# One output projection over all eight head pairs in a decoder trunk, without partial sums

## The chip, the core and the metric

The kernel runs on one core of a Trainium2 chip. The metric is device time of one launch in microseconds (us). The core has a matmul engine (PE, with its weight loads shown apart as PEld), three engines for elementwise work (DVE, ACT, POOL), and SP, which here issues nearly all DMAs between HBM and the on-chip SBUF. Matmuls write into PSUM, which has eight banks of 128 x 512 float32 here. Each engine works through its own instructions in order and waits on semaphores of the others.

## The reference, cut to what matters

Sequence 512, width 1024, 16 heads of 64, MLP width 4096, two layers. Layer 0 mixes by pooling, layer 1 by stick-breaking attention; each is followed by a squared-ReLU MLP.

```python
for layer in range(DEPTH):
    h = rms_norm(x, mix_pre_g[layer])
    if layer < N_A:
        m = pool_mixer(h, pool_w[layer], pool_scale[layer])
    else:
        q = jnp.matmul(h, w_q[j]).reshape(B, S, N_HEADS, HEAD_DIM).transpose(0, 2, 1, 3)
        o = stick_breaking_attention(q, k, v)
        m = jnp.matmul(o.transpose(0, 2, 1, 3).reshape(B, S, HD), w_o[j])
    x = x + rms_norm(m, mix_post_g[layer])
    h = rms_norm(x, mlp_pre_g[layer])
    x = x + rms_norm(sq_relu_mlp(h, w_up[layer], w_down[layer]), mlp_post_g[layer])
    if layer == N_A - 1:
        kv = jnp.matmul(rms_norm(x, kv_norm_g), w_kv)...
```

The change is in how `m = o @ w_o`, the norm behind it and the start of the second MLP are laid out.

## The kernel before, in words

Every float32 matrix product is made of three matmuls on rounded operands: each operand is split into a high part (an ACT cast, `hi`) and a low part (a DVE subtraction, `lo`), and `mm3` adds hi·hi, hi·lo and lo·hi. So each weight of 128 x 1024 costs one load, one ACT cast and one DVE subtraction before PE may use it. Where a weight is scaled by a norm's gains, there is a scaling ahead of that.

Weights reach PE in three ways. `weight` (line 139) loads and splits one on its way into a ring of four tiles (`place`, lines 171-189). Some are split beforehand during the first MLP (`split_apart`, lines 319-343: up to 31 steps, one behind each of its block products), stored to HBM as two parts (`keep_parts`) and later only loaded (`make`, lines 347-352); `SOON` says for how many of the eight head pairs the query and key weights go this way. The rest, listed in `LATE`, are loaded, scaled, split and, if marked `s`, stored during attention, at places that a table gives.

That table, `ATT_ORDER` (lines 55-66), is the order of attention written out by hand for PE, ACT, DVE, POOL and SP at once. A row is one head pair. `S` is the scores of a pair on PE, `G` their sigmoids on ACT, `X` a scan and `M` a product on DVE (for each of two heads), `Q`/`J` the projections of the next pair's queries and keys on PE and `q`/`j` their copies out of PSUM, `T` the transposes, `A` the product with the values, `a` its split into the tile `ohl`. `L`, `g`, `W`, `w`, `s` are a late weight's load, scaling (DVE), high part (ACT), low part (DVE) and store. `R` loads two rows of norm gains. `N`, `V`, `v`, `F` make the values in the first two rows.

The output projection before is done in three portions. `O00` to `O03` multiply the pairs 0 and 1 with their two weights for the four token tiles of 128, in the fifth pair's row; `o00` to `o03` copy the results to SBUF (`y`). `O10` to `O13` do pairs 2 and 3 in the last row, and `o1x` adds them to `y` on DVE. Behind the table the pairs 4 to 7 follow, tile after tile (lines 1337 to 1391), and are added to `y` once more. Each tile then goes through `Update` (lines 457 to 534): squares summed on ACT, a gain on POOL or DVE (`gained`), a power on POOL (`rstd`), `sums_added` into the residual `x` with squares of it, another power, `norm`, `transpose` on PE and a `split` into `xnh`/`xnl`, from which the second MLP's first matmuls read (`up_block`, line 816; the first four blocks take the first two token tiles first, and `need(2)`, `need(3)` transpose the other two at the fourth block).

`xn3` is one tile of three slots. A slot serves in turn as the place of an `Update`'s squares and normed rows, and of the high part of a late weight that is stored.

Two engines, PE and SP, run strictly in the order in which the table and the code behind it issue; in the two MLPs a scheduler at build time chooses the order.

## Time and profile before

| | us |
|---|---|
| three timed runs | 909.95, 913.77, 914.89 (median 913.77) |
| the profiled execution's own time | 911.04 |
| its span, first to last instruction | 909.2 |
| first MLP, roughly | 50 to 340 |
| attention rows (first scores to the eighth pair's scores) | 390.1 to 531.6 |
| second MLP, first matmul | 583.8 |

The profiled execution lies 2.7 us under the median and 1.1 us over the fastest of the three, and 1.8 us of it lie outside the span. In a row of the timeline the first number is the start, the second the duration; a matmul's duration includes its way through the array, so matmuls that follow each other closely overlap, and the distance of their starts tells the rate. In a row of the windows, each engine's busy time in that stretch is followed by its number of instructions, and PEclk is the share of full clock that PE was granted.

### The profile page before, as it was taken

How to read it: one execution, taken by the hardware profiler on the slowest of the kernel's cores; microseconds unless marked ns; L12 is line 12 of the kernel's file. 1: busy time of each engine (PE TensorE's matmuls, PEld its weight loads, DVE VectorE, ACT ScalarE, POOL GpSimd, SP SyncE). 2: the span in 40 equal slices, each digit the busy share in tenths (PEclk: the TensorE clock that was granted, in tenths of full speed). 3: DMA queues.
4: the chain of work that ended last, by engine and by line, in shares of the span. 5: the costliest groups of instructions: out<-in, count | busy, mean ns of one | idle time of the engine just before them, and what ended most of it. 6: DMA issues, size and time to landing. Idle time of an engine off the chain costs nothing.

```text
span 909.2 us, 11769 instructions
## 1 busy us (share of the span) xinstructions
PE 890.8 (98%) x4522; PEld 772.5 (85%) x4522; DVE 710.8 (78%) x728; ACT 546.0 (60%) x888; POOL 90.4 (10%) x86
## 2 busy tenths in 40 slices
PE   9999999999999999999999999799999999999996
PEld 7998888888888888888887877698888888888886
DVE  5956798987988965877986897764596876967956
ACT  6667757476896847366876873356554454544632
POOL 2100000000000014000000001211130310403103
PEclk9999999999999999999999999899999999999999
DMA  7443557377695823946412126032504243133102
GB/s 287 172 178 139 185 204 260 116 269 275 241 370 209 294 99 109 375 164 255 162 47 93 47 93 231 17 112 83 207 23 162 93 139 116 47 139 115 49 22 92
DMA packets 39725, 143.09 MB, mean 157 GB/s; under 512 B 4032, under 2 KB 4506, under 8 KB 39670
## 3 DMA queue, kind: packets, MB, share of 16 engines
q1 hardware_dynamic: 39522, 142.34, 42.9%
q8 instruction: 35, 0.57, 0.3%
q14 instruction: 20, 0.16, 0.1%
q10 hardware_dynamic: 148, 0.02, 0.0%
HBM read 117.17 MB, written 25.17 MB: 157 GB/s over the span
## 4 chain that ended last, share of the span: by engine, by line
PE 79%; DVE 8%; ACT 5%; DMA 3%; issue 3%; POOL 1%; SPq 0%; POOLq 0%; DVEq 0%; ACTq 0%
PE ps L708 24%; PE ps L822 13%; PE ps L821 13%; PE ps L823 13%; PE ps L1105 3%; DMA xn<-in_wdn 2%; PE ps L446 2%; PE ps L447 2%; PE ps L445 2%; PE ps L960 2%; PE ps L1195 2%; PE ps L1244 2%; DMA w<-kept 1%; PE ps L1254 1%; PE ps L936 1%
## 5 line engine op out<-in xcount | busy, mean ns | idle before, releaser
L708 PE MATMUL ps<-w,a 128*128 128x512 f32 x1176 | 266.7, 379 | 0.3 <-ACT a L407 0.3
L821 PE MATMUL ps<-xnh,w 128*128 128x512 f32 (+1 forms) x704 | 254.0, 363 | 2.5 <-ACT xnh L407 2.5
L822 PE MATMUL ps<-xnl,w 128*128 128x512 f32 (+1 forms) x704 | 254.0, 361 | 0.1
L823 PE MATMUL ps<-xnh,w 128*128 128x512 f32 (+1 forms) x704 | 253.8, 361 | 0.0
L708 PEld LDWEIGHTS ps<-w,a 128*128 128x128 f32 x1176 | 222.0, 189 | 32.3 <-ACT a L407 0.7
L821 PEld LDWEIGHTS ps<-xnh,w 128*128 128x128 f32 x704 | 133.5, 191 | 18.5 <-ACT xnh L407 3.1
L822 PEld LDWEIGHTS ps<-xnl,w 128*128 128x128 f32 x704 | 134.2, 191 | 15.6 <-DVE xnl L408 0.3
L823 PEld LDWEIGHTS ps<-xnh,w 128*128 128x128 f32 x704 | 134.2, 191 | 15.4
L153 DVE TENSOR_TENSOR w<-raw,w 128x1024 fp32r<-128x1024 f32 x56 | 68.4, 1221 | 55.2 <-ACT w L151 55.2
L151 ACT CAST w<-raw 128x1024 fp32r<-128x1024 f32 x56 | 58.5, 1045 | 81.6 <-PE ps L823 81.5
L717 DVE TENSOR_TENSOR y<-ps,y 128x512 f32<-128x512 f32 x124 | 82.7, 682 | 20.5 <-PE ps L708 20.5
L475 POOL TENSOR_TENSOR y<-y,grow 128x512 f32<-128x512 f32 x12 | 17.4, 1454 | 542.4 <-ACT xn L411 542.4
L407 ACT CAST w<-e 128x1536 fp32r<-128x1536 f32 (+1 forms) x30 | 41.8, 1393 | 42.5 <-DVE e L681 28.9
L407 ACT CAST a<-r 128x768 fp32r<-128x768 f32 (+1 forms) x60 | 47.0, 785 | 32.5 <-DVE r L662 17.5
L408 DVE TENSOR_TENSOR w<-e,w 128x1536 fp32r<-128x1536 f32 (+1 forms) x30 | 53.8, 1794 | 10.6 <-ACT w L407 10.4
L408 DVE TENSOR_TENSOR a<-r,a 128x768 fp32r<-128x768 f32 (+1 forms) x60 | 59.1, 984 | 0.0
L1228 DVE TENSOR_TENSOR_SCAN e<-u,begin 128x1280 f32<-128x1280 f32 x16 | 45.2, 2823 | 17.1 <-ACT u L1219 16.3
L411 ACT ACTIVATE xn<-y 128x512 f32<-128x512 f32 (+1 forms) x24 | 14.9, 621 | 50.9 <-DVE y L566 28.8
L408 DVE TENSOR_TENSOR w<-xn,w 128x1536 fp32r<-128x1536 f32 (+1 forms) x20 | 33.0, 1651 | 9.5 <-ACT w L407 9.3
L408 DVE TENSOR_TENSOR w<-w,w 128x1536 fp32r<-128x1536 f32 (+1 forms) x20 | 34.5, 1727 | 6.7 <-ACT w L407 6.7
L407 ACT CAST w<-xn 128x1536 fp32r<-128x1536 f32 (+1 forms) x20 | 27.8, 1390 | 18.9 <-PE ps L708 18.9
L740 ACT ACTIVATE r<-ps 128x512 f32<-128x512 f32 x56 | 33.0, 590 | 8.6 <-PE ps L823 8.6
(180 smaller groups left out, 1295.7 us busy)
## 6 DMA issues: line engine op xcount, KB each, us to landing
raw<-in_wup SPq DMA_DIRECT2D x62, 512.0 KB, 3.7
w<-kept SPq DMA_DIRECT2D x44, 512.0 KB, 6.0
w<-in_wdn SPq DMA_DIRECT2D x8, 1536.0 KB, 7.0
xn<-in_wdn SPq DMA_DIRECT2D x8, 1536.0 KB, 6.2
kept<-wx SPq DMA_DIRECT2D x20, 512.0 KB, 5.5
kept<-apart SPq DMA_DIRECT2D x16, 512.0 KB, 6.2
apart<-in_wv SPq DMA_DIRECT2D x10, 512.0 KB, 5.3
raw<-in_wdn SPq DMA_DIRECT2D x8, 512.0 KB, 4.5
```

Source lines behind the costliest of these rows:

```text
L151: nc.scalar.copy(hi, raw)
L153: nc.vector.tensor_tensor(out=lo, in0=raw, in1=hi.bitcast(F32), op=ALU.subtract)
L407: latest["act"] = nc.scalar.copy(hi, src)
L408: latest["dve"] = nc.vector.tensor_tensor(out=lo, in0=src, in1=hi.bitcast(F32), op=ALU.subtract)
L708: nc.tensor.matmul(bank, a[:, x, q, TS[t]], by_twos(w[:, z, q], NS[0]), start=start and q == 0 and k == 0, stop=q == self.n - 1 and k == 2 ...
L717: nc.vector.tensor_tensor(out=part, in0=bank, in1=part, op=ALU.add)
L740: nc.scalar.activation(split_up(r, 256), in_order(pu, 256), ACT.Relu)
L821: nc.tensor.matmul(pu[:, cols], wh[:, k, :], xh, start=k == 0, stop=False)
L822: nc.tensor.matmul(pu[:, cols], wh[:, k, :], xl, start=False, stop=False)
L823: nc.tensor.matmul(pu[:, cols], wl[:, k, :], xh, start=False, stop=k == KC - 1)
L1105: nc.tensor.matmul(bank, a[x][q], in_turn(w[q // 2][z][:, cols], 512), start=(i == 0 or not linked) and q == 0 and n == 0, stop=q == 3 and ...
L1228: nc.vector.tensor_tensor_scan(out=e[:, ::-1], data0=us[a][:, 1:][:, ::-1], data1=begin[:, ::-1], initial=0.0, op0=ALU.mult, op1=ALU.max,)
```

## The change

All eight pairs of a token tile now go into one PSUM sum for each half of the columns. `Z` followed by a tile and two pairs (`Z034`: tile 0, pairs 3 to 4) adds those pairs to the tile's two banks. Tiles 0 and 1 are begun in the last row of the table, up to pair 6, and hold four banks; behind the table pair 7 finishes them, and tiles 2 and 3 get all eight pairs in one go. The copies and additions into `y` are gone, as is the gain on POOL: `evacuate` squares the bank on ACT and multiplies the bank by the gain row on DVE into a tile `at`.

The weights of the projection must now stay until the end, so they get places of their own: `o0`, `o1` in the four `y` tiles, `o3`, `o4` in the columns of token tiles 2 and 3 of `xnh` and `xnl`, `o5` to `o7` in attention's own tiles, and only `o2` in the ring. In `xnh` a weight's row lies in eight pieces of 128 with a step of 512 elements; `by_twos` got a case for it. `SOON` goes from 4 to 5: `q4` and `k4` are split in the first MLP, whose steps go from 31 to 33 (one earlier, one later). In `LATE`, `up2` is no longer stored but kept in the ring, `up3` is stored at the very end, and `o0` and `o1` come early.

```diff
-    S1 G1 X10 M10 X11 Q2 M11 q2 W w s J2 A0 W j2 w s L a0 L g g T10 T11
-    S2 G2 X20 M20 X21 Q3 M21 q3 W w L J3 A1 W j3 w L a1 g g T20 T21
-    S3 G3 X30 M30 X31 Q4 M31 q4 W w L J4 A2 W j4 w L a2 T30 T31
-    S4 G4 X40 M40 X41 Q5 M41 q5 W w L J5 A3 W j5 w L a3 g g O00 W w L O01 o00 T40 o01 T41 O02 W w L o02 O03 g g o03
-    S5 G5 X50 M50 X51 Q6 M51 q6 W w L J6 A4 W j6 w L a4 T50 T51
+    S1 G1 X10 M10 X11 Q2 M11 q2 W w L J2 A0 W j2 w L a0 T10 T11
+    S2 G2 X20 M20 X21 Q3 M21 q3 J3 A1 j3 a1 g g T20 T21
+    S3 G3 X30 M30 X31 Q4 M31 q4 W w L J4 A2 W j4 w L a2 g T30 T31
+    S4 G4 X40 M40 X41 Q5 M41 q5 W w L g J5 A3 j5 W w L a3 g T40 T41
+    S5 G5 X50 M50 X51 Q6 M51 q6 W w L g J6 A4 j6 W w L a4 T50 T51
     S6 G6 X60 M60 X61 Q7 M61 q7 W w L J7 A5 W j7 w L a5 T60 W T61 w L
-    S7 G7 X70 M70 O10 W w L o10 X71 O11 M71 A6 o11 W a6 w O12 W T70 o12 w R O13 T71 o13 W w W w A7 a7""".split()
+    S7 A6 G7 X70 Z002 M70 W X71 w L Z102 M71 W T70 w a6 W w R W Z034 Z134 w L T71 W w L Z055 Z155
+    W w A7 Z066 Z166 a7 W w s""".split()
...
-SOON = 4
+SOON = 5
...
-    for w in "v0 v1 up2s up3s q4 k4 q5 k5 o0 o1 q6 k6 q7 k7 o2 o3 up0 up1 o4 o6 o5 o7".split()
+    for w in "v0 v1 o0 o1 q5 k5 q6 k6 q7 k7 o2 up0 o3 o4 up1 up2 o5 o6 o7 up3s".split()
...
+        if k in (("o", 0), ("o", 1)):
+            return tiles(work, (("y0", "y1"), ("y2", "y3"))[k[1]])
+        elif k in (("o", 3), ("o", 4)):
+            return [x[:, :, TS[k[1] - 1]] for x in (xnh, xnl)]
         elif k == ("o", 5):
-            return [att_pool[0].tile([P, D], F32R, tag="ohl", bufs=6, name=name("w")) for x in "hl"]
+            return tiles(att_pool[0], "kq")
...
-        if n < 2:
+        if n < 2 or upto["L"] > len(late) - 4:
             raw = wts.tile([P, D], F32, tag="raw", bufs=2, name=name("raw"))
...
+        if len(w.shape) == 3:
+            half = w[:, 4 * (cut.start // 512) :][:, : KC // 2]
+            return half.rearrange("p (j b) c -> p b c j", j=2)
         half = w[:, NS[cut.start // 512]].rearrange("p (j i) -> p i j", j=2)
...
-        steps = [n for n in range(1, 32)] if l == 0 else []
+        steps = [n for n in range(33)] if l == 0 else []
...
+        def out_product(t, cs, halves=range(2)):
+            for n in halves:
+                if (t, n) not in sums:
+                    sums[t, n] = ps()
+                for c in cs:
+                    if c not in wos:
+                        wos[c] = get(("o", c))
+                    (lh, ll), (wh, wl) = os[c], wos[c]
+                    mm3(
+                        sums[t, n], lh[:, TS[t]], ll[:, TS[t]], by_twos(wh, NS[n]), by_twos(wl, NS[n]),
+                        c == 0, c == PAIRS - 1,
+                    )
...
+            ups = [Update(t, gpost1, None, gpre=gpre1) for t in range(T)]
+
+            def evacuate(t, n):
+                up, bank = ups[t], sums.pop((t, n))
+                up.halves = (up.halves or []) + [ap.tile([P, 512], F32, tag="at", bufs=6, name=name("at"))]
+                up.just_square(n, bank)
+                latest["dve"] = nc.vector.tensor_tensor(
+                    out=up.halves[n], in0=bank, in1=gpost1[:, NS[n]], op=ALU.mult
+                )
+
+            for t in range(2):
+                for n in range(2):
+                    out_product(t, [PAIRS - 1], [n])
+                    evacuate(t, n)
+                ups[t].factor()
+            for t in range(2):
+                ups[t].sums_added()
+                ups[t].rstd()
+            for t in range(2):
+                ups[t].norm()
+            out_product(2, range(PAIRS), [0])
+            evacuate(2, 0)
+            out_product(2, range(PAIRS), [1])
+            ups[0].transpose()
+            evacuate(2, 1)
+            ups[2].factor()
+            out_product(3, range(PAIRS), [0])
+            ups[2].sums_added()
+            ups[1].transpose()
+            evacuate(3, 0)
+            ups[2].rstd()
+            ups[2].norm()
+            out_product(3, range(PAIRS), [1])
             fill(4)
...
```

The lines of `kernel.py` below attention's table move by up to 10: `L249` before is `L258` after, `L1155` is `L1165`, `L411` is `L418`.

First place: DVE in the fifth pair's row, from the low part of the next queries on. `w<-raw` is a late weight's low part, `gc` marks a scaling, `kl` is the low part of the next keys, `ohl` that of the attention output. Before:

```order
L1168 TENSOR_TENSOR q_4109<-ps_4083,q_4109 64x512 x2
L249 TENSOR_TENSOR w_4114<-raw_3777,w_4114 128x1024
L1155 TENSOR_TENSOR kl_2960<-ps_4119,k_4155 64x512 x2
L249 TENSOR_TENSOR w_4153<-raw_3823,w_4153 128x1024
L408 TENSOR_TENSOR ohl_4165<-ps_4144,ohl_4165 128x512
L223 TENSOR_TENSOR spare_3948<-spare_3948,gc 128x1024
L223 TENSOR_TENSOR late_3994<-late_3994,gc 128x1024
L249 TENSOR_TENSOR w_4184<-spare_3948,w_4184 128x1024
L249 TENSOR_TENSOR w_4259<-late_3994,w_4259 128x1024
```

And after:

```order
L1178 TENSOR_TENSOR q_4126<-ps_4100,q_4126 64x512 x2
L258 TENSOR_TENSOR w_4131<-spare_3630,w_4131 128x1024
L230 TENSOR_TENSOR late_3680<-late_3680,gc 128x1024
L1165 TENSOR_TENSOR kl_2988<-ps_4137,k_4171 64x512 x2
L258 TENSOR_TENSOR w_4178<-late_3680,w_4178 128x1024
L415 TENSOR_TENSOR ohl_4183<-ps_4162,ohl_4183 128x512
L230 TENSOR_TENSOR raw_3964<-raw_3964,gc 128x1024
```

One scaling has moved in front of `kl`, and the row ends with one scaling in place of four instructions.

Second place: ACT at the end of the table, where the tiles 0 and 1 are squared (`stat` with the smaller number is tile 0). The waits of an instruction stand behind it; `DMAHW` is a DMA's landing. Before:

```order
L411 ACTIVATE xn_80,stat_4831<-y_2987 128x512 [waits DVE_49] x2
L411 ACTIVATE xn_80,stat_4832<-y_2988 128x512 [waits DVE_49]
L411 ACTIVATE xn_80,stat_4831<-x_69 128x512 [waits DVE_49,Activation_49] x2
L411 ACTIVATE xn_80,stat_4832<-y_2988 128x512 [waits DVE_49]
L411 ACTIVATE xn_80,stat_4833<-y_2989 128x512 [waits DVE_49]
```

And after:

```order
L414 CAST ohl_4792<-ps_4771 128x512 [waits DVE_49,PE_49]
L249 CAST xn_80<-raw_4753 128x1024 [waits DMAHW1_49]
L418 ACTIVATE xn_80,stat_4800<-ps_4620 128x512 [waits PE_49]
L418 ACTIVATE xn_80,stat_4800<-ps_4630 128x512 [waits PE_49]
L418 ACTIVATE xn_80,stat_4801<-ps_4647 128x512 [waits DMAHW3_49,DVE_49,PE_49]
L418 ACTIVATE xn_80,stat_4801<-ps_4657 128x512 [waits PE_49]
L418 ACTIVATE xn_80,stat_4800<-x_69 128x512 [waits DVE_49,Activation_49] x2
```

The cast of `up3` into a slot of `xn3` now stands ahead of the squares, and the first square of tile 1, which writes the same slot, waits for a DMA: the store of that slot. The squares of tile 0's `x` stand behind it.

Third place: SP's queue at the end of the table, from the load of the gain rows (`grow`, `spare`) on; `kept<-` is a store, `w<-kept` its load, `in_wdn` the second MLP's first down weights. Before:

```order
L131 DMA grow_4766<-in_grow 128x1024
L131 DMA spare_4768<-in_grow 128x1024
L352 DMA w_4784<-kept_3601 128x1024 x2
L352 DMA w_4828<-kept_3647 128x1024 x2
L141 DMA raw_5199<-in_wup 128x1024
L141 DMA raw_5230<-in_wup 128x1024
L645 DMA w_5040<-in_wdn 128x2x1024
L131 DMA grow_7154<-in_grow 128x1024
```

And after:

```order
L132 DMA grow_4696<-in_grow 128x1024
L132 DMA spare_4698<-in_grow 128x1024
L223 DMA raw_4728<-in_wo 128x1024
L223 DMA raw_4753<-in_wup 128x1024
L142 DMA raw_5179<-in_wup 128x1024
L203 DMA kept_4797<-xn_80 128x1024
L203 DMA kept_4797<-raw_4753 128x1024
L142 DMA raw_5210<-in_wup 128x1024
L361 DMA w_4995<-kept_4797 128x1024 x2
L132 DMA grow_7134<-in_grow 128x1024
L655 DMA w_5020<-in_wdn 128x2x1024
```

Behind the last late loads now come the store and the reload of `up3`, and the first down weights stand behind the gain row `grow_7134`, whose place is read by the out projection's last `evacuate`.

More of the change, by code (lines that the diff above doesn't have):

```diff
@@ L231, in late_high @@
         else:
-            assert key[0] == "o" and key[1] > 3 or sum(k[0] != "o" or k[1] < 4 for k in made) < ahead
+            assert not in_ring(key) or sum(map(in_ring, made)) < ahead
             for y in queue:
@@ L359, in fill @@
         for _ in range(n):
-            if queue and sum(k[0] != "o" or k[1] < 4 for k in made) < ahead and (queue[0][0][0] != "dn" or dn_pool[0]):
+            if queue and sum(map(in_ring, made)) < ahead and (queue[0][0][0] != "dn" or dn_pool[0]):
                 if not any(x["key"] == queue[0][0] for x in late) or queue[0][0] in kept:
@@ L383, in trunk @@
                     want(("q", i), wq[i], gains(C_MIX_PRE1 * KC, KC))
-                elif what == "O" and part == 0:
-                    for c in range(2 * i, 2 * i + 2):
-                        want(("o", c), wo[c])
+            want(("o", 2), wo[2])
             direct = [x for x in queue[n:] if x[2] is not None]
@@ L1050, in quarter @@
         def quarter():
-            return ap.tile([P, 4, 256], F32, tag="ohl", bufs=6, name=name("s"))
+            return ap.tile([P, 4, 256], F32, tag="ohl", bufs=7, name=name("s"))
         def form(i):
@@ L1238, in transposed @@
                 c = 0
-                turned = ap.tile([P, S], F32, tag="at", bufs=8, name=name("at"))
+                turned = ap.tile([P, S], F32, tag="at", bufs=6, name=name("at"))
                 for s in tiles:
@@ L1260, in mixed_out @@
             if p < PAIRS - 1:
-                both = ap.tile([P, D], F32R, tag="ohl", bufs=6, name=name("ohl"))
+                both = ap.tile([P, D], F32R, tag="ohl", bufs=7, name=name("ohl"))
             else:
```

94 lines of the change are left out of this document (17 added, 77 removed).

## The prediction

> **What bounds the kernel now.** I read the page's busy shares and slices first, then the windows by stage, then PE's waits.
>
> ```profile
> PE 890.8 (98%) x4522; PEld 772.5 (85%) x4522; DVE 710.8 (78%) x728; ACT 546.0 (60%) x888; POOL 90.4 (10%) x86
> PE   9999999999999999999999999799999999999996
> PEclk9999999999999999999999999899999999999999
> ```
>
> PE is busy for 98% of the span. Its 4522 matmuls are the same arithmetic after the change (192 of them are the output projection, as 8 pairs x 4 tiles x 2 halves x 3), so the change can only gain where PE stood still or was slow, and can only lose by making it stand still elsewhere. In the slices there is one such place, the 26th, where PE and its clock fall together. The windows show it by stage; the first two run from a pair's scores to the next pair's:
>
> ```profile
> 450.30:467.50 17.20, 17.20 (x103) 14.10 (x101) 16.65 (x14) 13.82 (x30) 0.00 (x0) 1.00 0.18 62
> 467.50:497.30 29.80, 28.04 (x151) 23.20 (x150) 21.76 (x18) 20.63 (x41) 0.00 (x0) 1.00 0.24 81
> 573.60:588.00 14.40, 9.15 (x37) 7.33 (x37) 10.89 (x18) 5.54 (x15) 4.11 (x5) 0.76 0.00 0
> 150.00:200.00 50.00, 50.00 (x233) 43.77 (x233) 48.60 (x47) 30.17 (x35) 0.00 (x0) 1.00 0.50 179
> ```
>
> A plain pair takes 17.2 us of unbroken PE work, with DVE close behind at 16.65. The fifth pair (467.5) takes 29.8 because `O00` to `O03` lie in it, and the stretch from 573.6 has only 9.15 us of PE work, at 0.76 of the clock. In the first MLP (last row) PE never stops although DVE is busy for 48.6 of 50 us. PE's waits name the causes:
>
> ```profile
> PE ps L446 <- DVE w L249: 2.6, 2, 1.8
> PE ps L531 <- DVE xn L522: 2.6, 1, 2.6
> PE ps L821 <- ACT xnh L407: 2.5, 1, 2.5
> ```
>
> PE waits twice for the low part of an output weight (1.8 in the fifth pair, 0.8 in the last), once for the normed rows of tile 1 before their transposes, and once for the split of these before the second MLP.
>
> **What the change removes.** The rate of PE at the end of the projection, by starts:
>
> ```profile
> 572.92 0.38 PE L445 MATMUL ps<-w,ohl 128*128 128x512 f32 x1
> 573.13 0.38 PE L446 MATMUL ps<-w,ohl 128*128 128x512 f32 x1
> 576.37 1.32 PE L531 MATMUL ps<-ident,xn 128*128 128x128 f32 x8 [2.64 <-DVE xn L522]
> 578.24 0.63 PE L447 MATMUL ps<-w,ohl 128*128 128x512 f32 x1
> 578.67 0.63 PE L445 MATMUL ps<-w,ohl 128*128 128x512 f32 x1
> 583.79 0.60 PE L821 MATMUL ps<-xnh,w 128*128 128x256 f32 x3 [2.47 <-ACT xnh L407]
> 585.32 0.42 PE L822 MATMUL ps<-xnl,w 128*128 128x256 f32 x1
> 585.53 0.42 PE L823 MATMUL ps<-xnh,w 128*128 128x256 f32 x1
> 588.12 0.28 PE L821 MATMUL ps<-xnh,w 128*128 128x256 f32 x1
> 588.23 0.28 PE L822 MATMUL ps<-xnl,w 128*128 128x256 f32 x1
> ```
>
> A 512-column matmul comes every 0.215 us at full clock and every 0.43 after the 2.64 us wait; a 256-column one every 0.21, and every 0.11 once the clock is back. So the 37 instructions of the stretch 573.6 to 588.0 (the tail of one, 8 transposes, 9 matmuls of 512, 19 of 256) are worth 0.9 + 9 x 0.216 + 19 x 0.11 = 4.9 to 5.0 us, and 14.4 - 5.0 = **9.4 us** are lost there. Afterwards tiles 0 and 1 need only pair 7 behind the table (4 x 3 matmuls, 2.6 us), and tile 2's 48 matmuls (10.4 us) stand between them and the transposes of tile 0, and 24 more before those of tile 1. That is the cover for the chains of tiles 0 and 1.
>
> Fifth pair: 29.8 - 17.2 - 48 x 0.216 = **2.2 us** lost around `O00`, all of which goes, since the weights of pairs 0 and 1 are now split four rows before their use. Last pair: **0.8 us**. The copies and sums into `y` (8 on ACT, 16 on DVE) lie beside PE in both stages; I give them nothing. Removed in all: 12.4 us.
>
> **What it adds or moves.** *The 48 matmuls moved* from the fifth to the last row cost PE the same there. As fillers they cover the last pair: PE has 14 x 6 = 84 of them (18.1 us) there beside the pair's scores, transposes and value products, some 28 us in all. DVE has the 16.65 us of a plain pair, less the low parts of queries and keys (4 x 0.7), two late low parts and two scalings (4 x 1.2), plus seven late low parts and one split (9.2): 18. So DVE stays ahead, provided the late weights land. Their loads go through two buffers, each behind the low part of the weight before the last:
>
> ```profile
> raw<-in_wo SPq DMA_DIRECT2D x4, 512.0 KB, 3.3
> kept<-xn SPq DMA_DIRECT2D x2, 512.0 KB, 3.0
> w<-kept SPq DMA_DIRECT2D x44, 512.0 KB, 6.0
> w<-in_wdn SPq DMA_DIRECT2D x8, 1536.0 KB, 7.0
> ```
>
> The first two rows are medians of the attention stage, the others of the whole span. By my count `o7` is issued some 9 us before its first matmul and needs 3.3 to land, 1.0 of ACT and 1.2 of DVE: covered, and still at a landing of 6.
>
> *One scaling ahead of `kl`* (fifth and sixth pair). The third pair's `kl`, with two late low parts and no scaling before it:
>
> ```profile
> 448.53 1.39 DVE L1155 TENSOR_TENSOR kl<-ps,k 64x512 fp32r<-64x512 f32 x2
> 451.08 0.86 PE L1195 MATMUL ps<-kl,q 64*128 64x512 f32 x8
> 451.82 1.22 DVE L223 TENSOR_TENSOR spare<-spare,gc 128x1024 f32<-128x1024 f32 x1
> ```
>
> `kl` ends at 449.92 and PE wants it at 451.08, so 1.16 us are spare and the scaling takes 1.22: 0.1 us in the fifth pair, 0.2 in the sixth, which starts a little later. I take 0.3 (bounds 0 and 2 x 1.2). The rows in between carry no more on DVE than the third pair did (two low parts, two scalings).
>
> *Chains of tiles 0 and 1.* Durations:
>
> ```profile
> L411 ACT ACTIVATE xn<-y 128x512 f32<-128x512 f32 x23 | 14.5, 630 | 49.9 <-DVE y L566 27.9 <-DVE y L1353 22.0
> L1353 DVE TENSOR_TENSOR y<-ps,y 128x512 f32<-128x512 f32 x8 | 5.4, 682 | 2.3 <-PE ps L447 2.3
> L497 DVE SCALAR_TENSOR_TENSOR x<-y,stat,x 128x512 f32<-128x512 f32 x23 | 16.3, 747 | 2.1 <-POOL stat L424 1.8
> L424 POOL TENSOR_TENSOR stat<-stat,mhalf 128x1 f32<-128x1 f32 x20 | 11.1, 554 | 35.1 <-DVE stat L415 33.7 <-DVE stat L483 1.3
> 574.58 2.40 DVE L522 SCALAR_TENSOR_TENSOR xn<-x,stat,spare 128x512 f32<-128x512 f32 x2 [0.66 <-POOL stat L424]
> 574.51 1.26 POOL L475 TENSOR_TENSOR y<-y,grow 128x512 f32<-128x512 f32 x1
> 592.60 1.41 DVE L522 SCALAR_TENSOR_TENSOR xn<-x,stat,spare 128x512 f32<-128x512 f32 x2 [0.66 <-POOL stat L424]
> ```
>
> Count from the first matmul of pair 7 behind the table. Tile 0 is squared by 2.3 us. Tile 1's squares wait for the store of `up3`'s high part: its load goes out some 5 us ahead, its cast ends near -0.7, and the store lands 3.0 later, at 2.5 to 3.2. The four products with the gains end at 5.2, `sums_added(0)` (2 x 0.75) at 6.8, its squares and the sum at 7.7, `sums_added(1)` at 9.2, its squares and sum at 10.2, then `norm(0)`: with no gain on POOL beside it I take the 1.41 us row, not the 2.40 one, so 11.6. PE reaches the transposes of tile 0 at 2.6 + 10.4 = 13.0. So it waits for nothing, with 1.4 us to spare. If the store takes 6 us, as the reloads do over the whole span, tile 1 is 3 us later and PE waits 1.6. I take **0.5** (bounds 0 and 2.6, the wait it replaces). Tile 3, whose normed rows came at 594.0 before, behind tile 2's norm on DVE, now finds that norm past: square, gain, powers and norm take 0.8 + 0.7 + 0.2 + 0.7 + 1.5 + 0.9 + 0.9 + 1.5 = 7.2 us, while `need(3)` stands 9.4 us of first-half matmuls later.
>
> *The first down weights* go out behind `grow_7134`, near 28 us on the same count; they need 7.0 to land and are wanted near 42: nothing.
>
> *Two more weights split in the first MLP.* Each costs DVE a subtraction, ACT eight scalings and a cast:
>
> ```profile
> L342 DVE TENSOR_TENSOR apart<-apart,wx 128x1024 f32<-128x1024 f32 x10 | 12.1, 1215 | 0.0
> L162 ACT ACTIVATE apart<-apart,gc 128x128 f32<-128x128 f32 x56 | 17.4, 389 | 0.0
> L341 ACT CAST wx<-apart 128x1024 fp32r<-128x1024 f32 x10 | 10.4, 1041 | 0.0
> ```
>
> That is 2.4 us of DVE and 2 x 4.2 of ACT near the end of this MLP, hidden by PE's work; the steps of the values come one product earlier, into the stretch where DVE has 1.4 us of 50 free. I take 0 (bounds 0 and 2.4).
>
> *The read of `o3` and `o4`* from `xnh`, two elements 4 KB apart instead of 1 KB: no row shows it. The nearest row, the 1 KB read above, runs at 0.216, and 512-column matmuls at half the clock at 0.43. I take 0 (bounds 0 and 48 x 0.215 = 10.3).
>
> **Sum.** -12.4 + 0.3 + 0.5 = -11.6. The profiled execution's 911.04 becomes 899.4; from the median of 913.77 it would be 902.2. The 1.8 us outside the span stay. The profiled execution lies inside the three runs' spread, 2.7 under the median, so I take the middle of the two, **900.8 us**.
>
> **The rivals.** *1. PE waits for tile 0's transposes and the clock falls again* (late store of `up3`, ACT queued behind it). For it: the wait in the order of ACT. Against: stores landed in 3.0 us in this stage. Price: 2.6 us of wait as before, and the clock: 0.76 over 14.4 us is 6.9 us at half of it, 3.4 us lost. So +2.1 + 3.4: 906.3. The Trainium skill, "TensorE: Matmul & The Clock Gate", section "HAM oscillation — how this bites in real kernels", asks for no idle gap over about 3.4 us; by that such a wait would cost itself alone, 902.9. This trace is stricter: the clock fell behind 2.64 us.
>
> *2. The first MLP pays for the splits*, up to 2.4 us: 903.2. For it: DVE's 48.6 of 50. Against: even there PE lost nothing.
>
> *3. The 4 KB read runs at half rate*: +10.3, 911.1, no measurable change. Against it: steps of 1 KB (572.92 to 573.13) and of 512 B (`xnh` itself, 588.12 to 588.23) are both at full rate.
>
> *4. Slower than before.* The scheduler reorders PE in the first MLP around the shifted steps; a block product that PE now reaches before its operands waits for a pair of DVE subtractions, 1.9 + 1.1 us. Six such waits, of 35 products, are 18 us: 918.8, which is slower than 913.77 by 5.0; from six on it decides. Against it: these products waited 0.3 us in total before:
>
> ```profile
> L708 PE MATMUL ps<-w,a 128*128 128x512 f32 x1176 | 266.7, 379 | 0.3 <-ACT a L407 0.3
> L408 DVE TENSOR_TENSOR w<-e,w 128x1536 fp32r<-128x1536 f32 x24 | 46.5, 1936 | 2.7 <-ACT w L407 2.5
> L408 DVE TENSOR_TENSOR a<-r,a 128x768 fp32r<-128x768 f32 x48 | 50.9, 1059 | 0.0
> ```
>
> **How the numbers follow.** Forecast 62% (897 to 904), rival 1 15% (902 to 908), rival 2 9% (901 to 905), rival 3 7% (908 to 913), rival 4 4%, something unnamed 3%. Eight in ten lie between 896.5 and 908. A change of 0.5%, 4.6 us, is about what a measurement of this kernel can tell from none. Under 909.2 lie the forecast, rivals 1 and 2 and a third of rival 3: faster 0.87; same 0.08; slower 0.05.
>
> **What would show it.** Right: PE's waits `<- DVE xn` and `<- ACT xnh` are gone, PEclk is 9 in every slice, the fifth pair takes 17.2 to 17.5 us, and from the eighth pair's scores to the second MLP's first matmul it takes about 54 us (52.2 before, and 10.4 more work). Wrong: starts of the matmuls on `xnh` with `ohl` more than 0.22 apart (rival 3), PE idle before 340 us (2 and 4), a wait at `L541` (1), or a wait for a late weight in the last row.

## The result and the profile after

| kernel | median us (runs) | kernel before beside it | ratio, 95% interval |
|---|---|---|---|
| changed | 906.61 (7) | 914.89 (7) | 0.9914 [0.9889, 0.9940] |
| changed, a second time | 905.00 (6) | 913.07 (11) | 0.9912 [0.9891, 0.9933] |

The changed kernel is faster by 0.9%, some 8 us. The forecast was 900.8, 4 to 6 us under what came. The profiled execution took 907.11 us (span 905.3), against 911.04 (909.2) of the kernel before: 3.9 less. That of before lies 1.3 under the median of all 63 runs of it on record (912.35), and that of the changed kernel 1.7 over the median of its 13 (905.39), so the two profiles show less than the medians do; these two medians are 7.0 apart. One profiled execution further down, of the kernel with its splits later, ran at a granted clock of 0.753 throughout and took 1161.55 us; the comparisons leave it out, and its profile was taken a second time.

The page of the changed kernel, PE's share and the slices (the 26th is the one that fell before):

```profile
PE 891.3 (98%) x4522; PEld 770.6 (85%) x4522; DVE 700.1 (77%) x714; ACT 546.0 (60%) x896; POOL 84.4 (9%) x82
PE   9999999999999999999999999999999999999996
PEclk9999999999999999999999999999999999999998
```

No slice but the last, in which PE ends, shows a fall of the clock. That says less than it seems: a slice is 22.6 us long, and 3 us at half the clock take only 0.07 off it. PE's waits are there (total, times, longest):

```profile
PE ps L1205 <- DVE kl L1165: 1.5, 2, 0.9
PE ps L877 <- POOL warm L839: 1.3, 1, 1.3
PE ps L718 <- ACT a L414: 1.0, 2, 0.5
PE ps L456 <- DVE dn L154: 0.8, 1, 0.8
PE ps L1205 <- ACT at L1256: 0.4, 2, 0.2
PE ps L1115 <- DMA w<-kept: 0.4, 1, 0.4
PE ps L718 <- DVE a L415: 0.4, 1, 0.4
...
```

The three waits of before (`w`, `xn`, `xnh`) are gone. In their place stand `kl` in the attention, and `a` and `dn` in the first MLP. The windows of the fourth to seventh pair, each from its first scores to the next pair's, and of the transition (busy time and instructions by engine, then the granted clock):

```profile
454.50:471.70 17.20, 17.20 (x104) 14.10 (x101) 15.53 (x13) 13.83 (x30) 0.00 (x0) 1.00 0.05 15
471.70:489.70 18.00, 17.44 (x104) 14.13 (x101) 16.47 (x14) 12.49 (x26) 0.00 (x0) 1.00 0.21 74
489.70:508.95 19.25, 18.08 (x101) 14.13 (x101) 16.80 (x14) 13.84 (x30) 0.00 (x0) 1.00 0.17 56
508.95:528.60 19.65, 19.40 (x100) 15.30 (x101) 14.87 (x12) 15.17 (x34) 0.00 (x0) 0.91 0.16 55
567.50:581.90 14.40, 14.40 (x77) 12.75 (x76) 9.84 (x17) 4.80 (x13) 1.92 (x3) 1.00 0.16 55
```

The transition (last row) is unbroken at full clock: 14.40 of 14.40, where 9.15 stood before. But the fifth, sixth and seventh pair take 18.00, 19.25 and 19.65 us in place of 17.2. By stage, from the starts of the first scores of a pair and of the second MLP's first matmul:

| stage | before | changed |
|---|---|---|
| start to the first pair's scores | 390.1 | 394.3 |
| first pair's scores to the eighth's | 141.5 | 134.3 |
| eighth's scores to the second MLP | 52.2 | 53.2 |
| the rest of the span | 325.4 | 323.5 |

The second row should have fallen by 10.4 (the 48 matmuls that moved) + 2.2 = 12.6 and fell by 7.2: 5.4 us are lost in the three pairs. The third row took in the 10.4 and grew by 1.0, so 9.4 are gained there, and 1.9 more in the last row, where the second MLP no longer begins at half the clock (in the kernel before its first 256-column matmuls came every 0.21 us until 588 and every 0.11 from there). Gained: 2.2 + 9.4 + 1.9 = 13.5. Lost: 5.4 + 4.2 in the first MLP = 9.6. Net 3.9.

The losses begin on VectorE. Its timeline in the fifth pair:

```profile
485.76 1.23 DVE L258 TENSOR_TENSOR w<-spare,w 128x1024 fp32r<-128x1024 f32 x1
486.90 1.22 DVE L230 TENSOR_TENSOR late<-late,gc 128x1024 f32<-128x1024 f32 x1
488.15 1.39 DVE L1165 TENSOR_TENSOR kl<-ps,k 64x512 fp32r<-64x512 f32 x2
...
494.55 2.82 DVE L1238 TENSOR_TENSOR_SCAN e<-u,begin 128x1280 f32<-128x1280 f32 x1 [1.90 <-ACT u L1229]
```

The scaling (L230) stands ahead of `kl`, and PE waits for `kl`, 0.6 us here and 0.9 in the next pair. That is the wait the prediction priced. But ScalarE waits for the same scaling:

```profile
488.15 1.05 ACT L249 CAST w<-late 128x1024 fp32r<-128x1024 f32 x1 [1.21 <-DVE late L230]
489.22 0.59 ACT L414 CAST ohl<-ps 128x512 fp32r<-128x512 f32 x1
489.70 2.62 ACT L1256 COPY at<-ps 128x512 f32<-128x512 f32 x6
492.14 0.68 ACT L1229 ACTIVATE u<-ps 128x511 f32<-128x511 f32 x1
```

The high part of the scaled weight holds ScalarE for 1.21 us; the copies of the transposed tiles (`at`) and the next pair's sigmoids (`u`) stand behind it. They start 2.4 us after the scores (489.70), and VectorE's scan, idle for 1.90, late after them.

### The profile page after: what moved, and what is told of

The parts are those of the page before. It is cut to its first block, busy times and chain, and to the rows that moved or that the text cites. A ratio compares the mean times of both kernels' runs of the same rounds, so it can differ in the third digit from the quotient of the medians.

```text
span 905.3 us, 11765 instructions
## 1 busy us (share of the span) xinstructions
PE 891.3 (98%) x4522; PEld 770.6 (85%) x4522; DVE 700.1 (77%) x714; ACT 546.0 (60%) x896; POOL 84.4 (9%) x82
## 4 chain that ended last, share of the span: by engine, by line
PE 80%; DVE 7%; ACT 5%; DMA 4%; issue 2%; SPq 0%; POOL 0%; POOLq 0%; DVEq 0%; ACTq 0%
PE ps L718 22%; PE ps L831 13%; PE ps L832 13%; PE ps L833 13%; PE ps L1115 3%; PE ps L455 3%; PE ps L457 3%; PE ps L456 3%; DMA xn<-in_wdn 2%; PE ps L1205 2%; PE ps L970 2%; PE ps L1264 2%; PE ps L1254 1%; DMA w<-kept 1%; DMA raw<-in_wdn 1%
## 5 line engine op out<-in xcount | busy, mean ns | idle before, releaser
L154 DVE TENSOR_TENSOR w<-raw,w 128x1024 fp32r<-128x1024 f32 x56 | 70.9, 1268 | 50.2 <-ACT w L152 50.2
L415 DVE TENSOR_TENSOR w<-e,w 128x1536 fp32r<-128x1536 f32 (+1 forms) x30 | 54.8, 1827 | 9.1 <-ACT w L414 8.9
L415 DVE TENSOR_TENSOR a<-r,a 128x768 fp32r<-128x768 f32 (+1 forms) x60 | 60.1, 1002 | 0.6 <-ACT a L414 0.6
L485 POOL TENSOR_TENSOR y<-y,grow 128x512 f32<-128x512 f32 x8 | 12.4, 1550 | 345.0 <-ACT xn L418 345.0
L415 DVE TENSOR_TENSOR w<-xn,w 128x1536 fp32r<-128x1536 f32 (+1 forms) x20 | 33.0, 1649 | 9.0 <-ACT w L414 8.7
L415 DVE TENSOR_TENSOR w<-w,w 128x1536 fp32r<-128x1536 f32 (+1 forms) x20 | 32.9, 1645 | 6.6 <-ACT w L414 6.6
L414 ACT CAST w<-w 128x1536 fp32r<-128x1536 f32 (+1 forms) x20 | 27.8, 1391 | 14.5 <-PE ps L718 14.1
```

Of the source, the lines that this page charges most:

```text
L154: nc.vector.tensor_tensor(out=lo, in0=raw, in1=hi.bitcast(F32), op=ALU.subtract)
L414: latest["act"] = nc.scalar.copy(hi, src)
L415: latest["dve"] = nc.vector.tensor_tensor(out=lo, in0=src, in1=hi.bitcast(F32), op=ALU.subtract)
```

## The experiments

All times are medians in us, ratios against the kernel before, run beside it on the same chip. "By the profile" means from one profiled execution of each kernel.

**1. The scalings behind the keys.** Four scalings in the third pair, two at the end of the fifth, none ahead of a `kl`:

```diff
-    S2 ... q3 J3 A1 j3 a1 g g T20 T21
-    S3 ... q4 W w L J4 A2 W j4 w L a2 g T30 T31
-    S4 ... q5 W w L g J5 A3 j5 W w L a3 g T40 T41
-    S5 ... q6 W w L g J6 A4 j6 W w L a4 T50 T51
+    S2 ... q3 g J3 A1 j3 g a1 g g T20 T21
+    S3 ... q4 W w L J4 A2 W j4 w L a2 T30 T31
+    S4 ... q5 W w L J5 A3 W j5 w L a3 g g T40 T41
+    S5 ... q6 W w L J6 A4 W j6 w L a4 T50 T51
```

> The changed kernel with the scalings of late weights moved in the order of the attention: four in the third pair (one ahead of the keys' product, one behind the keys' split, two behind the mixture, as the kernel before placed scalings and splits together), none in the fourth, two at the end of the fifth, none in the sixth; nothing is left out. Theory A: the 5.4 us which the sixth, seventh and eighth row of scores come late (18.01 + 19.25 + 19.69 = 56.95 us for three pairs against 3 x 17.17 = 51.5) stem from a scaling that stands ahead of the split of the keys on VectorE, directly (kl late, 0.8 and 0.7 us of waits) and through ScalarE, whose high part of the late weight waits for the scaling and pushes the copies behind it. Then these three pairs take 17.1 to 17.3 us each, the waits on kl go, and the time falls by 4.5 to 5.5 us against the changed kernel: about 901.5, 0.985 of the time before. Rival B: VectorE is full over these rows and a scaling costs there wherever it stands. Then the third pair grows by about 2 to 3 us, the sum of the pairs stays within 1.5 us of 161, and the time stays at 905 to 907, 0.991.

Measured: 901.91 against 911.92, 0.9883 [0.9859, 0.9907]; all three pairs are 17.20 to 17.23 us apart, and the waits on `kl` and `at` are gone. ScalarE in the fifth pair of this kernel:

```profile
485.83 0.59 ACT L414 CAST ohl<-ps 128x512 fp32r<-128x512 f32 x1
486.34 2.83 ACT L1256 COPY at<-ps 128x512 f32<-128x512 f32 x6
489.04 0.63 ACT L1229 ACTIVATE u<-ps 128x511 f32<-128x511 f32 x1
```

Nothing waits, and the sigmoids start 1.3 us behind the scores (487.7), not 2.4. Theory A holds: it was the place of the scalings, not their number.

**2. One scaling alone ahead of the keys**, in a kernel without the other losses (experiment 8 below, 898.28):

```diff
-    S4 ... W w L J5 A3 W j5 w L a3 g g T40 T41
-    S5 ... W w L J6 A4 W j6 w L a4 T50 T51
+    S4 ... W w L J5 A3 W j5 w L a3 g T40 T41
+    S5 ... W w L g J6 A4 j6 W w L a4 T50 T51
```

> The kernel with packed splits and scalings behind the keys (898.3 measured; rows of scores 17.2 us apart), in which one scaling alone is put back ahead of the keys: the last one, in the sixth pair, between the low part of a late weight and the keys' product. Nothing is left out. It measures the price of one scaling at that place, for which the prediction had 0.2 us, with a bound of 2.4. Theory A (two queues): VectorE brings the keys' low part 0.8 to 1 us late, which TensorE waits for at the next scores, and ScalarE, whose high part of the late weight waits for the scaling, brings the copies behind it late, so that the sigmoids of the next pair and the row after it end late too. Then the row of the sixth pair takes 17.9 to 18.2 us, the row of the seventh 17.8 to 18.5, and the time grows by 1.3 to 2.3 us, to 899.6 to 900.6, 0.987 of the time before. Rival B (VectorE alone): the row of the sixth pair takes 17.9 to 18.2 us and the next again 17.2; the time grows by 0.7 to 1, to 899. Rival C (the prediction's term): under 0.3 us in all, 898.3 to 898.6.

Measured: 900.94 against 912.31, 0.9868 [0.9849, 0.9887]; the sixth pair's row takes 18.04, the seventh's 19.74. By the profiles the one scaling costs 899.3 - 895.9 = 3.4 us, by the medians 2.7, against 0.2 in the prediction. Theory A's sizes for the next row were still too low, because the clock fell as well; the windows behind the wait (the clock is the seventh figure):

```profile
502.00:505.00 3.00, 2.20 (x13) 1.16 (x12) 2.60 (x3) 2.98 (x7) 0.00 (x0) 1.00 0.26 102
505.00:508.00 3.00, 3.00 (x14) 2.55 (x13) 0.31 (x1) 3.00 (x10) 0.00 (x0) 0.56 0.50 165
508.00:511.00 3.00, 3.00 (x14) 2.55 (x13) 2.87 (x2) 2.62 (x8) 0.00 (x0) 0.87 0.02 5
```

**3. The high part moved behind the sigmoids** in the kernel of experiment 2, to tell ScalarE's share from VectorE's:

```diff
-    S5 ... W w L g J6 A4 j6 W w L a4 T50 T51
-    S6 G6 X60 M60 X61 Q7 M61 q7 W w L J7 ...
+    S5 ... W w L g J6 A4 j6 a4 T50 T51
+    S6 G6 X60 W M60 X61 w L Q7 M61 q7 W w L J7 ...
```

> The kernel with one scaling ahead of the keys in the sixth pair (900.9 measured; rows of the sixth and seventh pair 18.04 and 19.74 us), in which the high and the low part of the weight that is scaled there move behind the sigmoids and the first scan of the next pair; nothing is left out. Theory A (two queues): ScalarE no longer waits 1.21 us for the scaling ahead of the copies, so the sigmoids start 1.2 to 1.5 us behind the scores and not 2.5. Then the row of the sixth pair stays at 17.9 to 18.1, for the keys' low part is as late as it was, but the row of the seventh falls to 17.2 to 17.5, the clock stays at 1.00 there, and the time is 899.0 to 899.6. Rival B: the row of the seventh pair is late because its scores began late, or because the clock fell behind TensorE's wait for the keys. Then it stays above 18.5 us and the time at 900.5 to 901.2.

Measured: 905.10 against 913.07, 0.9914 [0.9895, 0.9934]: slower than either theory had it, for the edit made a wait of its own. The moved weight is the next key's, and PE now stood for its low part (the wait as PE's timeline shows it, and the sigmoids on ScalarE):

```profile
515.21 0.48 PE L833 MATMUL ps<-xnh,w 128*128 128x512 f32 x1 [3.94 <-DVE w L258]
```

```profile
504.33 0.60 ACT L1229 ACTIVATE u<-ps 128x511 f32<-128x511 f32 x1 [0.91 <-PE ps L1205]
```

The row of the sixth pair is 18.04 again, so `kl` costs its 0.84 whatever ScalarE does. The sigmoids start 1.3 us behind the scores (503.0), as theory A said, and no longer 2.5. What the seventh row would take without the new wait can't be read from this run, so it does not decide between its two theories.

**4 to 7. Where the first MLP loses 4.2 us.** By the starts of the matmuls, PE's gaps there in the changed kernel are near 231 (0.8 us), 281 to 292 (1.7) and 328 to 334 (2.1); before there was one of 0.6 at 289. The steps of the splits began one product earlier, two weights were added, and the steps end later. Three edits of single numbers or places; 7 is a second profile of 4:

```diff
# 4, changed kernel: begin as before, end two products later than before
-        steps = [n for n in range(33)] if l == 0 else []
+        steps = [n for n in range(1, 34)] if l == 0 else []
# 5, kernel before: begin one product earlier
-        steps = [n for n in range(1, 32)] if l == 0 else []
+        steps = [n for n in range(31)] if l == 0 else []
# 6, changed kernel: the two weights added are not scaled and not split
-                scaled(raw)
-            elif m == 2:
+                x[3] = raw.bitcast(F32R) if k[1] == 4 else scaled(raw)
+            elif m == 2 and k[1] != 4:
```

> The changed kernel with the 33 steps of the splits in the first MLP begun at the second product of blocks, as in the kernel before, and ended two products later than there; nothing is left out. The changed kernel reaches its first scores 4.2 us later than the kernel before (394.3 against 390.1), with gaps at 231, 282, 291 and 328 to 336 us. Theory A: the start one product earlier puts the steps of the value forms beside busier products and makes the gaps at 231 to 291. Then those gaps go, the first scores come at 391 to 392.5, and the time falls by 2 to 3 us, to about 904, 0.988 of the time before. Rival B: the two weights more cost the time, wherever the steps stand. Then the gaps stay or move behind 300 us, the first scores stay at 393.5 to 395.5, and the time stays at 906 to 908, 0.991 to 0.993.

> The kernel before with its 31 steps of the splits in the first MLP begun one product of blocks earlier, as in the changed kernel, and with its own twelve weights; nothing is left out. Theory A: the earlier start alone costs. Then the first scores come at 392 to 393.5 in place of 390.1, gaps stand at 231 to 291 us, and the time grows by 2 to 3 us, to 1.002 to 1.004 of the time before. Rival B: the two added weights cost. Then the first scores come at 389.8 to 390.8 and the time is that before within 0.7 us, 0.999 to 1.001.

> The changed kernel, in which the two weights that were added to the splits of the first MLP (the query's and the key's of the fifth pair) are loaded and stored in their steps, but neither scaled nor split: eight products by a gain column on ScalarE each, one cast on ScalarE and one subtraction on VectorE each are left out, and what is stored stands for both parts. The attention's work stays as it is. Theory A: the earlier start costs, not the added work. Then the first scores stay at 393.5 to 394.5, the time at 906 to 907, 0.991 of the time before. Rival B: the added work on ScalarE and VectorE costs. Then the gaps at 328 to 336 us go, the first scores come at 390 to 391.5, and the time falls by 3 to 4 us, to about 903, 0.987. If both share it, the first scores lie near 392.3.

| kernel | median us | ratio, interval | first scores at |
|---|---|---|---|
| 4 splits later | 910.60 | 0.9977 [0.9959, 0.9994] | 397.0 (second profile) |
| 5 before, splits earlier | 913.80 | 1.0011 [0.9996, 1.0025] | 390.7 |
| 6 two not split | 904.95 | 0.9911 [0.9889, 0.9933] | 392.6 |

In 4 neither theory came, in 5 rival B did, and in 6 both share the loss. The earlier start alone costs no more than the interval (5: 0.6 us by the profile). A later start does not mend it, it adds 4 us by the medians and 2.8 by the profiles (4). The added splits are a part of it: without them the gaps at 328 to 334 are gone (6), though those at 281 to 292 stay (2.7). The second profile of 4 was to say where its 4 us lie:

> A second profile of the changed kernel with its 33 steps begun at the second product (910.6 measured against 906.6), since that of the first run shows no waits in the first MLP. Theory A: the last store leaves one product later than in the changed kernel, the third down weight's load is issued behind it, later than 317.7 us, and TensorE waits for down weights and the products behind for 4 to 6 us between 325 and 340 us, against 1.9. Rival B: the loss of 4 us lies between 200 and 320 us, at the products of blocks.

It took 909.99 us. Its gaps at 231 and 281 are gone, as theory A of 4 had said, and only 0.6 us remain at 289, as in the kernel before. But between 326 and 337 PE loses 6.8: 1.2 at products of blocks, 2.8 waiting for a down weight, 2.8 on matmuls 0.43 us apart behind it. So the end of the splits is what costs, as theory A had it, but not by a late load: that was issued at 315.12. ScalarE's cast of the third down weight waited for something else, as the trace's row says:

```profile
330.02 1.99 ACT L152 CAST dn<-raw 128x1024 fp32r<-128x1024 f32 x2 [3.31 <-DMA kept<-apart]
```

The third down weight's parts lie in the buffers of the splits (`apart`), which the last store, issued at 322.60, left only when it had landed. In the changed kernel that store leaves at 314.61, and the load is late. Its SyncE timeline:

```profile
314.61 0.32 SPq L203 DMA_DIRECT2D kept<-apart  x1
316.77 0.90 SPq L361 DMA_DIRECT2D w<-kept  x2
317.72 1.30 SPq L142 DMA_DIRECT2D raw<-in_wdn  x2
```

The last two down weights' loads (`raw<-in_wdn`) stand behind the store of the last split weight, which waits for VectorE until 314.6, and behind reloads that wait in turn. They were issued at 313.45 before and at 317.72 now. ScalarE cast the third down weight at 321.10 before; now:

```profile
327.21 1.04 ACT L152 CAST dn<-raw 128x1024 fp32r<-128x1024 f32 x1 [4.06 <-DMA raw<-in_wdn]
```

PE waited for its low part, the `dn` of the list above. The gaps at 281 to 292 have another origin. VectorE stood for 4.59 us at the head of its queue until the group's 1.5 MB of down weights, issued at 268.4, had landed, with an operand of the running products (L415) behind the waiting instruction:

```profile
278.32 1.76 DVE L691 TENSOR_TENSOR e<-xn,w 128x1536 f32<-128x1536 f32 x1 [4.59 <-DMA xn<-in_wdn]
279.99 1.75 DVE L415 TENSOR_TENSOR w<-w,w 128x1536 fp32r<-128x1536 f32 x1
```

The order is not new. In the kernel before the same two instructions stand in it, the load was issued at 266.98, and the wait was shorter:

```profile
276.17 1.76 DVE L681 TENSOR_TENSOR e<-xn,w 128x1536 f32<-128x1536 f32 x1 [3.89 <-DMA xn<-in_wdn]
```

PE's loss at 281 to 292 follows this wait through the runs: 0.6 us at waits of 3.89 (before) and 3.94 (4), 1.3 at 4.50 (5), 1.7 at 4.59 (changed), 2.7 at 5.57 (6). Of these kernels the two whose steps begin at the second product have the short waits. Why the load lands later beside an earlier start, no run shows.

**8 and 9. The steps packed.** The second half of the value forms begins at its seventh step in place of the eighth (two forms are made in place, so that no buffer is missing), and the first load at the fifteenth, so 32 steps do in place of 33. Experiment 8 begins at the first product and ends where the kernel before ended; 9 is the same one product later. Both keep the scalings behind the keys.

```diff
-            names = "B0 D3 A1 E2 C4 G3".split() if h == 0 else "B0 D1 A2 E3 C4 G1".split()
+            names = "B0 D3 A1 E2 C4 G3".split() if h == 0 else "B0 D1 A2 E1 C4 G2".split()
-                steps[8 * h + n].extend(jobs)
+                steps[7 * h + n].extend(jobs)
-        if apart and n >= 16:
+        if apart and n >= 15:
-            raw = buffer((0, 2, 1, 3, 4, 0, 2, 1, 3, 4, 0, 2, 1, 0)[n - 16])
+            raw = buffer((0, 3, 1, 2, 4, 0, 3, 1, 2, 4, 0, 1, 2, 0)[n - 15])
-        steps = [n for n in range(33)] if l == 0 else []
+        steps = [n for n in range(32)] if l == 0 else []
```

In 9 the last line is `range(1, 33)`.

> The kernel with the scalings behind the keys (901.9 measured), in which the splits of the first MLP take 32 steps in place of 33: the second half of the value forms begins one product of blocks earlier, in other buffers, and the loads of the other weights with it, so that the last store leaves one product earlier, at the place where the kernel before had it; the first step stays at the first product. Nothing is left out. Theory A: the end of the splits costs, not their number: the last two stores stand on SyncE's queue ahead of the down weights, whose third came to ScalarE at 327.21 and not at 321.1, and TensorE lost some 1.9 us between 327 and 334. Then these gaps go or fall under 0.7 us in sum, and the time falls by 1 to 2 us against 901.9, to 900 to 901. Rival B: the number of splits costs, on VectorE and ScalarE, wherever they stand. Then gaps of the same sum appear elsewhere between 200 and 335 us, and the time stays within 0.6 us of 901.9 or grows.

> The same 32 packed steps, begun at the second product of blocks as in the kernel before, so that they end where the changed kernel's do. Theory A (the place of the last stores decides): the gaps of 327 to 334 us stay at 1.5 to 2 us, the time is that of the kernel with the scalings behind the keys, 901.3 to 902.5, and 1 to 2 us over the packed steps that begin at the first product. Rival B (the start decides): the gaps at 231 to 291 go, and the time falls below 901.

Measured: 8 takes 898.28 against 911.79, **0.9854 [0.9841, 0.9868]**, 3.6 us under the 901.91 of experiment 1; 9 takes 900.84, 0.9884 [0.9870, 0.9898]. All that PE waits for in 8:

```profile
PE ps L877 <- POOL warm L839: 1.3, 1, 1.3
PE ps L1115 <- DMA w<-kept: 0.4, 1, 0.4
PE ps L1205 <- DVE ohl L415: 0.3, 1, 0.3
```

The first scores come at 390.1, as in the kernel before, with the two weights more. So their work costs next to nothing; the place of the steps costs. The time is 1.7 us under theory A's range, for the gaps at 281 to 292 went too, which theory A had not said. VectorE's order there:

```profile
273.64 1.76 DVE L415 TENSOR_TENSOR w<-w,w 128x1536 fp32r<-128x1536 f32 x1 [0.42 <-ACT w L414]
277.71 1.76 DVE L691 TENSOR_TENSOR e<-xn,w 128x1536 f32<-128x1536 f32 x1 [2.31 <-DMA xn<-in_wdn]
```

The load lands as late as ever (277.71), but the operand stands ahead of the wait, not behind it. In 9 it stands behind again, VectorE waits 6.12 us, and the gaps are back with 3.3 us; 329 to 334 cost 1.5 in it. 9's median is 0.5 under its range for theory A and so within the time of rival B (below 901), but what B says of the gaps did not come.

**10. The down weights' loads on GpSimd's queue**, with the unpacked 33 steps of experiment 1:

```diff
-        nc.sync.dma_start(raw, src)
+        (nc.gpsimd if dn_pool[0] is not None and not upto['L'] else nc.sync).dma_start(raw, src)
```

> The kernel with the scalings behind the keys and 33 unpacked steps (901.9 measured), in which the raw loads of the first MLP's four down weights are issued on GpSimd's queue in place of SyncE's; nothing is left out. Theory A (order on SyncE's queue): the third load was issued at 316 to 318 us because the stores of the last two split weights, which wait for VectorE, and the reloads behind them stand ahead of it; on a queue of its own it goes out as soon as its buffer is free, near 314, and lands by 321. Then the gaps from 327 to 334 us (1.8 us in sum) go, those at 280 to 291 stay, and the time falls by 1.2 to 2 us, to 900 to 900.7. Rival B (the DMA engines are full): they are busy for 0.87 to 1.03 of 304 to 328 us, so the load lands at 325 or later all the same, the gaps stay and the time stays at 901.3 to 902.5.

Measured: 898.94 against 912.31, 0.9852 [0.9837, 0.9867], 3.0 under experiment 1 by the medians, more than theory A had, and 1.6 by the profiles. Issue and cast of the third weight:

```profile
314.93 0.55 POOL L142 DMA_DIRECT2D raw<-in_wdn  x1 [12.05 <-DVE dn L154]
324.20 1.05 ACT L152 CAST dn<-raw 128x1024 fp32r<-128x1024 f32 x1 [1.60 <-DMA raw<-in_wdn]
```

The load went out only 1.2 us earlier than in experiment 1 (316.08) and still took over 8 us to land. The order delays the issue, as theory A says; that the full DMA engines (0.93 busy from 304 to 328 us) delay the landing, as B says, fits but is not shown. PE first needs the weight at 327, so 324.20 is enough, and the gaps from 327 on are gone, while 1.2 us at 281 to 291 stay. Theory A decides.

**11. The cover of the transition taken away.** The transposes of tile 0 go ahead of the second half of tile 2's products:

```diff
             evacuate(2, 0)
+            ups[0].transpose()
             out_product(2, range(PAIRS), [1])
-            ups[0].transpose()
             evacuate(2, 1)
```

> The changed kernel with the transposes of tile 0 ahead of the second half of tile 2's products (24 matmuls of 512 columns) instead of behind them; nothing is left out. Theory A: the transition no longer waits because the 24 matmuls, 5.2 us, lie over the end of tile 0's and tile 1's norm; the spare is about 1 us for tile 1's norm, more for tile 0's. Tile 0's norm ends near 568.5 and TensorE reached the transposes at 569.65, so it would now reach them at 564.45 and wait for the norm for 3.5 to 4.5 us, with the clock falling to half behind it for up to 1.7 us more: the time grows by 3.5 to 6 us, to 910 to 912.5, 0.995 to 0.998 of the time before. Rival B: the cover isn't what took the wait away, since the norms end early by themselves (squares spread over the last pair). Then the wait is under 1 us and the time stays at 906 to 907.5.

Measured: 912.02 against 911.79, 0.9998 [0.9988, 1.0008]: the whole gain of the change is gone. PE's wait, and the windows behind it:

```profile
PE ps L541 <- DVE xn L532: 3.8, 1, 3.8
```

```profile
565.00:570.00 5.00, 2.60 (x12) 2.15 (x13) 4.15 (x8) 3.05 (x8) 1.23 (x2) 0.84 0.01 3
570.00:575.00 5.00, 5.00 (x21) 4.24 (x20) 1.00 (x2) 0.00 (x0) 0.00 (x0) 0.82 0.00 0
```

Theory A holds: the 24 matmuls are the cover, and without them a wait and half the clock return, in the same place as in the kernel before.

**12. The changed kernel a second time.**

> The changed kernel unaltered, a second time, beside the other runs' kernel before: its first comparison gave 0.9914 with a kernel before of 914.9, while that stood at 911.8 to 912.3 in the three comparisons since. If those runs were high by chance, the ratio comes out at 0.993 to 0.9945, as the profiles (3.9 us of 911) and the price of the two repairs (4.7 and 3.6 us from 0.9854) have it; if not, at 0.991 to 0.992. The profile tells which of the waits in the first MLP come back: those at 327 to 334 us should, as in every kernel whose last store leaves at this place, and those at 280 to 291; the one at 231 need not.

0.9912: the guess that the first ratio was too good falls. Its profile has the gaps at 327 to 334 (1.7 us) and 281 to 291 (1.7) again, one of 0.6 at 231, and pairs five to seven at 18.01, 19.25 and 19.59. That the profiles show 3.9 us and the two comparisons 8 comes from where the profiled executions lie in the scatter of their kernels (909.24 to 916.54 before, 903.28 to 908.32 changed); what makes that scatter stays open.

## Why the prediction was right, and where it was not

It said faster, and its wide range (896.5 to 908) holds the time. The narrow one of the forecast itself (897 to 904) does not: 900.8 was 4 to 6 us too low. Faster came for the reason given, the transition that is now covered. That the time stayed within the wide range is in part luck: two terms put at 0.3 and 0 cost 9.6 us by the profile, and 906.6 lies where rival 1 (902 to 908) would have put it, which did not come. Rival 2 named one of the two places, with too small a price; the other was in no rival. Of the signs, PE's two waits went as said, but the fifth pair took 18.0 us, not 17.2 to 17.5, and PE was idle before 340 us, the sign of rivals 2 and 4. Point by point:

- **"-12.4 removed": right.** 13.5 came. The fifth pair's 2.2 are there. Behind the eighth pair's scores 9.4 + 1.9 = 11.3 came, where the prediction had 9.4 for the transition and 0.8 for the last pair; the 1.1 more are not traced. Experiment 11 shows that without the named cover the whole gain is lost.
- **"One scaling ahead of `kl`, I take 0.3 (bounds 0 and 2 x 1.2)": this step failed.** 5.4 us by the profile, 4.7 by the repair; one alone 2.7 to 3.4 (experiment 2). Two things were wrong in it. It priced `kl` against the first matmul that reads it (451.08) and so found 1.16 us to spare. In the changed kernel PE waits for `kl` already ahead of the scores' first matmul, which reads only `k` and `q`; before, and in experiments 1 and 8, that matmul waits for ScalarE alone. The kernel before, and the changed one behind the fifth pair:

```profile
450.33 0.82 PE L1195 MATMUL ps<-k,q 128*128 128x512 f32 x4
```

```profile
489.68 0.47 PE L1205 MATMUL ps<-k,q 128*128 128x512 f32 x1 [0.56 <-DVE kl L1165]
```

  Before, it came 0.4 us behind the end of `kl` (449.92), in the changed kernel 0.15 behind it (489.54). So of the 1.16 us some 0.25 were to spare, and a scaling of 1.22 brings the scores up to 1 us late; a row with this loss alone lost 0.8 (18.04 in experiments 2 and 3). Why the program has its wait there in these rows, no run shows. Second, the step looked at VectorE's queue alone. The scaling has another reader, ScalarE's high part. In the table before, this `W` stood ahead of the keys' copies (`A3 W j5`); now it stands behind them and right behind its scaling (`j5 W`), and the sigmoids of the next pair queue behind it. Of the 5.4 us, `kl` is 2 x 0.8 and the clock 1.5 (below). The rest, some 2.3, goes with the late sigmoids by the rows of ScalarE and VectorE; experiment 1 removes it with the others, and no run separates it. The bound counted each scaling's own time and neither of these.
- **"Two more weights split in the first MLP: I take 0 (bounds 0 and 2.4)": mis-sized.** 4.2 us by the first profile, 3.4 by the second (first scores at 393.5), 3.6 by the repair. The step counted engine time, which indeed costs nothing (experiment 8). It left out what each step puts on SyncE's queue, the buffers that the last step holds, and that a load which lands later holds up what stands behind it on VectorE (1.7 us of PE's gaps, where the kernel before had 0.6). Rival 2 named the place, not the price. Rival 4's many waits did not come: PE's waits for `a` are three, 1.4 us in all.
- **"Chains of tiles 0 and 1: 0.5": 0 came, and the chain was sized well.** From the first matmul of pair 7 (556.70) on, the store landed at 3.7, not 2.5 to 3.2, `norm(0)` ended at 11.9 (568.58), where the prediction had 11.6, and PE came to the transposes at 13.0, as it said. So 1.1 us were to spare:

```profile
569.43 0.38 PE L457 MATMUL ps<-h,ohl 128*128 128x512 f32 x1
569.65 1.04 PE L541 MATMUL ps<-ident,xn 128*128 128x128 f32 x8
```

Rival 1 did not come.

- **"The read of `o3` and `o4`: 0": right**, rival 3 falls; the matmuls on `xnh` with `ohl` are 0.216 us apart, as all others:

```profile
566.41 0.38 PE L455 MATMUL ps<-xnh,ohl 128*128 128x512 f32 x1
566.63 0.38 PE L456 MATMUL ps<-xnl,ohl 128*128 128x512 f32 x1
```

- **Late loads and first down weights: covered**, as said; PE waited for neither.

With the three terms at their measured size the sum is 911.04 - 13.5 + 5.4 + 4.2 = 907.1, the profiled time. It closes because all three are read from the same two profiles; the evidence for the two losses is their repair, 906.61 to 901.91 (experiment 1) to 898.28 (experiment 8).

## What to carry to other kernels

When an instruction is moved ahead on one engine, list all its readers, and for each the queue that it holds up while it waits: here the second reader seems to have cost more than the one that the move was checked against. Look up in the changed program where the consumer waits: that can be ahead of the first instruction that reads the result. A transfer's price is its place in the issuing queue: two stores that cost no engine anything delayed by some 4 us a load that PE needed. A wait at the head of an in-order queue costs whatever ready work stands behind it, so a shift of unrelated steps can make or remove it.
